# Gate rows of the last layer taken as row sums and carried through memory, and half of the last MLP's first products in plain fp32

## The chip, the cores and the metric

The kernel runs on one core of one Trainium2 chip. The metric is the device time of one execution in microseconds (us), lower is better. The median of three runs of the kernel before is 1636.49 us, from 1636.38 to 1636.56.

## The reference, cut to what matters

Two layers over 256 latent and 256 context tokens of width 1024. Layer 0 mixes tokens by a convolution module, layer 1 by a bidirectional mLSTM with four heads; behind each mixer stands an MLP with a squared ReLU. Every sub-layer is modulated and gated by six vectors that a linear map of the conditioning vector gives.

```python
sh1, sc1, g1, sh2, sc2, g2 = adaln(c[:, None, :], ada_w[i], ada_b[i])   # silu(c) @ w + b, cut in six
u = modulate(h, sh1, sc1)                                               # h * (1 + sc1) + sh1
...
h = layer_norm(ALPHA * h + g1 * y, ln1_g[i], ln1_b[i])
h = layer_norm(ALPHA * h + g2 * sq_relu_mlp(modulate(h, sh2, sc2), mlp_w1[i], mlp_w2[i]), ln2_g[i], ln2_b[i])
```

In layer 1 only the latent stream is needed at the end. What the change touches are g1 and g2 of layer 1, the denominators of the mLSTM's heads, and the first quarter of `u @ w1` of layer 1's MLP.

## The kernel before

All weights are float32 in memory. For the tensor engine each weight block is split into a high part `wh`, rounded to the engine's fp32r type by ScalarE (`split`, L155), and a low part `wl`, the rest, by VectorE (L156). A product is then three fp32r products: high by high, high by low, low by high (`mm3` L186 to L190, `mm3t` L224 to L226). In layer 1's MLP the activations `u2` lie as [high | low], 512 columns wide, so that one product with `wh` over 512 columns and one with `wl` over 256 columns do the same (`wide` L202, `wides` L213); `joined` adds the two halves. A product in plain fp32 (no split) is one instruction in the program and two matmul records in the trace.

Weights come through SyncE's queue in blocks of 1 MB into `raw`, a tile with three buffers (L149). A buffer is free when the split that reads it is done. The tile framework orders each engine's instructions with a scheduler of its own, which may move work far ahead of the place where it is written; `issue_after` and pinned order bind it.

**The six vectors of layer 1.** Units of 512 outputs are computed from `ada_w`. Units 0 to 3 and 6 to 9 (sh1, sc1, sh2, sc2) are made by VectorE (`AdaV.step`, L434): a multiply and row sum over a transposed weight block `ar` from `adaT_w`, two halves to a column of 128 outputs. Units 4 and 5 (g1) go in the same class another way (L442, L444): VectorE accumulates the weight rows scaled by the conditioning vector, and `AdaV.row` (L453 to L463) sums over the partitions with four products by a matrix of ones and adds the result to G1, which was loaded with the bias. Units 10 and 11 (g2) are made by the tensor engine in the last seam (`Ada.mm`, L356, 16 plain fp32 products 32 columns wide), and `gate2` (L2027 to L2032) spreads them over the partitions with four products.

**The attention stage.** `attend(h)` forms the numerators of head h, `denominators(h)` (L1711 to L1723) four products by a column of ones, an absolute value on ScalarE and a maximum and reciprocal on VectorE. It is called within `attend(h)` behind the first numerator. At the end of `attend(h)` stand eight transposes (L1823).

**The last seam.** When the residual `R` of the mLSTM is done (L1902, L1903), it is normalised (`ln1_rows`, L1927), transposed in four turns of four blocks (`turn`, L1961), and scaled and split into `u2` (L1967, L1978 to L1983). The 16 products of g2 are pinned between the turns. Then the first four output blocks of w1 run together (`wides`, eight steps of the contraction, in each four products over 512 and four over 256 columns), then blocks 4 and 5 (their weights split ahead into `wx`), 6, 7, and then w2's 16 half blocks of this chunk.

Of the kernel before, what the change touches and what calls it, by code (L numbers as in the profile page):

```python
# [71 lines left out]
def hybrid_kernel(ctx: ExitStack, tc: tile.TileContext, xT, vecs_d, taps_d, bdw_d, ada0_w, ada_w, adaT_w, wg_d, pw1a, pw1, pw2, w1_0, w2_0,  # L72
# [131 lines left out]
    def wides(pss, ws, rhs):  # L204

        n = rhs[0][0].shape[-1] // 2
        for kt in range(8):
            for low in (1, 0) if kt == 7 else (0, 1):
                for ps, w in zip(pss, ws):
                    w_, x_, o_ = kcol(w, kt)[low], rhs[kt][0], ps  # L210
                    if low:
                        x_, o_ = x_[:, :n], ps[:, :n]
                    nc.tensor.matmul(o_, w_, x_, start=kt == 0 and not low, stop=kt == 7 and not low)  # L213
# [23 lines left out]
    def gemm_steps(w_ap, groups, rhs, n, epi, ko=0, pre=None, spare={}, ahead=False):  # L237
# [25 lines left out]
        if ko:  # L263
            ws, pss = [], []
            for m in range(ko):
                g = groups[m // 2]
                if m not in pre:
                    if (g, 0) not in raws:
                        raws[g, 0] = raw_load(w_ap[g, 0])
                    pre[m] = split_w(raws[g, 0][:, (m % 2) * 1024:(m % 2 + 1) * 1024])  # L270
                ws.append(pre[m])
                pss.append(psum("mm" if m < 3 else "cv")[:, :n])
            if len(rhs[0]) == 1:
                wides(pss, ws, rhs)
# [138 lines left out]
    class AdaV:  # L413
# [4 lines left out]
        def __init__(self, l, units, streams, rows=()):  # L418
            self.l, self.units, self.streams, self.i, self.acc = l, list(units) + list(rows), streams, 0, []
            self.ncol, self.loads = len(units), []  # L420

        def step(self):
            n, kt = divmod(self.i - len(self.loads), DT)
            if n == len(self.units):
                return
# [3 lines left out]
            if n < self.ncol:  # L429
                b, half = divmod(kt, 2)  # L430
                col = 4 * self.units[n] + b
                for s in self.streams:
                    o = ada[self.l][:, col, s:s + 1]
                    nc.vector.tensor_tensor_reduce(tmp("S") if s == 0 else w, w, crow[s][half], 1.0,  # L434
                                                   o if half else V(f"ada_b{self.l}", col),
                                                   op0=ALU.mult, op1=ALU.add, accum_out=o)
                return
            if kt == 0:
                self.acc.append(tmp("S"))
            a, c = self.acc[-1], cs[:, kt, 14 + self.streams[0]:15 + self.streams[0]]  # L440
            if kt == 0:
                nc.vector.tensor_scalar(a, w, c, None, op0=ALU.mult)  # L442
            else:
                nc.vector.scalar_tensor_tensor(a, w, c, a, op0=ALU.mult, op1=ALU.add)  # L444

        def load(self):
            n, kt = divmod(self.i, DT)
            u = self.units[n]
            w = adp.tile([P, 512], F32, tag="ar", name=nm("ar"), bufs=2)
            nc.sync.dma_start(w, adaT_w[u - 2 * (u > 5), kt // 2, kt % 2] if n < self.ncol  # L450
                              else ada_w[self.l, u, kt // 4, :, kt % 4 * 512:kt % 4 * 512 + 512])
            self.i += 1
            return w  # L453

        def row(self, i, dst):

            parts = tmp("E", F32R), tmp("E", F32R)
            split(*parts, self.acc[i])
            ps = psum(("mm", "fl")[i])
            for k, part_ in enumerate(parts):  # L460
                nc.tensor.matmul(ps, ones_r, part_, start=k == 0, stop=k == 1)
            with tc.high_priority(-300):
                nc.vector.tensor_tensor(dst, ps, dst, op=ALU.add)  # L463
# [804 lines left out]
    ada_n1, ada_n2 = AdaV(1, range(4), (0, 1)), AdaV(1, range(6, 10), (1,), (4, 5))  # L1268
# [3 lines left out]
    def each1(c, m, s):  # L1272
        if c == 0 and m == 7 and s != 0:
# [3 lines left out]
            for k in range(4):  # L1277
                with tc.issue_after(loaded[0]):
                    nc.sync.dma_start(crow[k // 2][k % 2],
                                      rows_d[6 + k // 2:7 + k // 2, k % 2 * 512:k % 2 * 512 + 512].broadcast_to([P, 512]))  # L1280
# [167 lines left out]
    for _ in gemm_steps(wv, range(8), xm, T, v_epi):  # L1448
# [9 lines left out]
        if vstep > ET:  # L1458
            ada_n2.step()
# [176 lines left out]
    for p in range(2):  # L1636
        pair(p)
    rx = raw_load(wo[0, 0, 0])
# [72 lines left out]
    def denominators(h):  # L1711

        den, es = psum("ln"), sums[h]
# [20 lines left out]
    def gate_o(h):  # L1734

        for d in range(2):
# [5 lines left out]
            for q in range(4):  # L1742
# [3 lines left out]
                for i in range(2):  # L1746
                    w = ws[i] if ws else split_w(raw[:, i * 1024:(i + 1) * 1024])
                    for t in range(2):
# [6 lines left out]
                        if q == 3 and i == 1:  # L1755
                            og[h, d, t] = o_ = OG()
                            nc.vector.tensor_tensor(o_, pss[t], bo, op=ALU.add)
                            nc.scalar.activation(o_, o_, AF.Sigmoid)
# [13 lines left out]
    def attend(h):  # L1772
# [5 lines left out]
        for t in range(2):  # L1778
            for d in range(2):
# [7 lines left out]
                if h not in rden:  # L1787
                    denominators(h)
                    if h == H - 1:
                        with tc.issue_after(mark["abs"]):  # L1790
                            nc.scalar.activation(con.tile([P, 1], F32, name=nm("warm")), eps, AF.Sqrt)
# [25 lines left out]
        for jp in range(2):  # L1817
            tr = psum("ln")
            for jj in range(2):
                j = 2 * jp + jj  # L1820
                for t in (1, 0):
# [3 lines left out]
                    if jj == 0 and t == 1:  # L1825
                        lead = a.ins
            y = og[h, 1, jp]
# [109 lines left out]
    for main, side, per in Z.att:  # L1937
# [7 lines left out]
        for _ in side:  # L1945
            pass
    for g_ in range(2):
        rx = raw_load(w1_1[g_, 0])
        for m in range(2 * g_, min(2 * g_ + 2, 3 + Z.pre4)):
            pre1[m] = split_w(rx[:, (m % 2) * 1024:(m % 2 + 1) * 1024])  # L1950
    ca, cb = comb(1, "ln1_g1", "ln1_b1", "sc2", "sh2", (1,))
    ada_n3 = Ada(1, 10, 2)
    fold_r = con.tile([P, 16], F32R, name="fold_r")
    nc.vector.tensor_copy(fold_r, fold)
    u2 = [X(F32R) for _ in range(DT)]

    def turn(t, g_, tag="ln"):

        tr = psum(tag)
        for i in range(4):  # L1960
            nc.tensor.transpose(tr[:, i * P:(i + 1) * P], R[:, t, g_ * 512 + i * P:g_ * 512 + (i + 1) * P], ident)  # L1961
        return tr

    def lows(y, t, g_):
        for i in range(4):
            f = 4 * g_ + i
            nc.vector.tensor_tensor(u2[f][:, C + t * P:C + (t + 1) * P], y[:, i * P:(i + 1) * P],  # L1967
                                    u2[f].bitcast(F32)[:, BLK[t]], op=ALU.subtract)

    def ln1(tr, t, g_, vector=False, low=True, y=None, blocks=range(4)):  # L1970

        ts = BLK[t]
        y = y or tmp("SL"[vector])
        for i in blocks:
            f, sl = 4 * g_ + i, slice(i * P, (i + 1) * P)
            for o_ in (u2[f][:, ts], y[:, sl]):
                if vector:
                    nc.vector.tensor_scalar(o_, tr[:, sl], ca[:, 1, f:f + 1], cb[:, 1, f:f + 1],  # L1978
                                            op0=ALU.mult, op1=ALU.add)
                else:  # L1980
                    nc.scalar.activation(o_, tr[:, sl], AF.Identity, scale=ca[:, 1, f:f + 1], bias=cb[:, 1, f:f + 1])
            if low:
                nc.vector.tensor_tensor(u2[f][:, C + t * P:C + (t + 1) * P], y[:, sl], u2[f].bitcast(F32)[:, ts],  # L1983
                                        op=ALU.subtract)
        return y

    def ada_unit(blocks, kts=range(DT)):
        pin[0] = True
        ada_n3.mm(blocks, kts)
        pin[0] = False  # L1990

    units = [ada_load(1, 10)]
    with tc.issue_after(loaded[0]):
        units.append(ada_load(1, 11, PW))
    tr0 = turn(0, 0)
    y0 = ln1(tr0, 0, 0, low=False, blocks=range(2))
    tr1 = turn(0, 1, "cv")

    scaled = ln1_rows(1, True)
    with tc.issue_after(roots[0]):  # L2000
        ln1(tr0, 0, 0, low=False, y=y0, blocks=(2, 3))
    ada_unit(units[0])
    ada_unit(units[1], range(4))
    with tc.issue_after(scaled):
        lows(y0, 0, 0)
        ln1(turn(1, 0), 1, 0)
        tr2 = turn(1, 1)
        ada_unit(units[1], range(4, 8))
# [225 lines left out]
```

## Time and profile before

| what | value |
|---|---|
| median of three runs | 1636.49 us |
| the profiled execution | 1636.4 us |
| its span, first to last instruction | 1634.7 us |
| granted tensor engine clock, mean | 0.999 |
| busy: tensor engine, its weight loads | 99%, 83% |
| busy: VectorE, ScalarE, GpSimd | 66%, 45%, 1% |
| instructions | 22791 |

Times in the timeline count from the span's start. PE is the tensor engine's matmul, PEld its weight load, DVE VectorE, ACT ScalarE, SPq SyncE's queue. A timeline row gives start, length, engine, line, operation, written and read tiles, partitions by columns, and how many instructions are merged in it. The length of a matmul holds its latency; in a merged row the pitch is (row's length less one instruction's) by (count less one). The 1.7 us between the span and the execution's time lie outside the instructions.

### The profile page before, as it was taken

The page shows a single profiled execution, that of the slowest core. Times are in us where ns is not written, and L with a number is a line of the kernel's source. Part 1 is how long each engine was busy: PE and PEld are TensorE (multiplying, and loading weights), DVE is VectorE, ACT ScalarE, POOL GpSimd, SP SyncE. Part 2 cuts the span into 40 slices and gives each one's busy share as a digit, 9 for nine tenths or more (in the row PEclk, how much of TensorE's full clock was granted, in tenths as well). Part 3 has the DMA queues.
Part 4 walks back from the last instruction along what each step waited for, and adds up shares of the span by engine and source line. Part 5 has one row for each costly group of instructions (what it writes and reads, how often), then busy time and mean ns, then how long its engine had stood idle before and what let it go on. Part 6 is the DMA issues. An engine that isn't in the chain of part 4 may idle for free.

```text
span 1634.7 us, 22791 instructions
## 1 busy us (share of the span) xinstructions
PE 1624.8 (99%) x8758; PEld 1352.7 (83%) x8758; DVE 1071.5 (66%) x2013; ACT 732.9 (45%) x1176; POOL 15.3 (1%) x67
## 2 busy tenths in 40 slices
PE   9999999999999999999999999999999999999998
PEld 6675998888888998877787899888888888878887
DVE  7697896886635877862234643453489876786777
ACT  4314763232324585552223532443478654555453
POOL 0000000000000000000000000000000000000001
PEclk9999999999999999999999999999999999999999
DMA  9766323556523078697563622342556565675552
GB/s 359 257 219 245 104 104 135 172 195 213 174 91 142 23 236 258 199 302 229 194 226 139 248 106 103 130 180 104 177 204 229 209 223 206 235 294 182 181 198 85
DMA packets 88124, 306.87 MB, mean 188 GB/s; under 512 B 12844, under 2 KB 31184, under 8 KB 60112
## 3 DMA queue, kind: packets, MB, share of 16 engines
q1 hardware_dynamic: 65552, 289.12, 50.3%
q10 hardware_dynamic: 22464, 16.30, 3.1%
q8 instruction: 69, 1.13, 0.3%
q14 instruction: 39, 0.32, 0.1%
HBM read 287.52 MB, written 17.86 MB: 187 GB/s over the span
## 4 chain that ended last, share of the span: by engine, by line
PE 98%; DVE 1%; ACT 0%; issue 0%; DVEq 0%
PE mm L186 18%; PE mm L189 18%; PE mm L190 18%; PE mm L202 10%; PE mm L226 3%; PE mm L224 3%; PE mm L225 3%; PE cv L226 2%; PE cv L224 2%; PE cv L225 2%; PE fl L356 1%; PE ln L224 1%; PE ln L225 1%; PE ln L226 1%; PE fl L225 1%; PE fl L224 1%
## 5 line engine op out<-in xcount | busy, mean ns | idle before, releaser
L156 DVE TENSOR_TENSOR wl<-raw,wh 128x1024 fp32r<-128x1024 f32 x344 | 419.0, 1222 | 262.8 <-ACT wh L155 260.4
L155 ACT CAST wh<-raw 128x1024 fp32r<-128x1024 f32 x344 | 359.4, 1053 | 455.2 <-PE mm L189 275.3
L189 PE MATMUL mm<-u,wh 128*128 128x512 f32 (+1 forms) x802 | 288.7, 361 | 0.0
L186 PE MATMUL mm<-u,wh 128*128 128x512 f32 (+1 forms) x674 | 239.4, 356 | 0.0
L190 PE MATMUL mm<-u,wl 128*128 128x512 f32 (+1 forms) x674 | 238.2, 355 | 0.0
L189 PEld LDWEIGHTS mm<-u,wh 128*128 128x128 f32 x802 | 151.2, 189 | 23.0 <-issue 0.8
L186 PEld LDWEIGHTS mm<-u,wh 128*128 128x128 f32 x674 | 127.2, 189 | 20.5 <-issue 2.4
L190 PEld LDWEIGHTS mm<-u,wl 128*128 128x128 f32 x674 | 127.1, 189 | 18.5 <-issue 0.8
L186 PE MATMUL mm<-xm,wh 128*128 128x512 f32 x256 | 100.2, 391 | 0.0
L190 PE MATMUL mm<-xm,wl 128*128 128x512 f32 x256 | 99.6, 389 | 0.0
L186 PE MATMUL mm<-hid,wh 128*128 128x512 f32 (+1 forms) x256 | 93.0, 364 | 0.0
L189 PE MATMUL mm<-hid,wh 128*128 128x512 f32 (+1 forms) x256 | 92.8, 362 | 0.0
L190 PE MATMUL mm<-hid,wl 128*128 128x512 f32 (+1 forms) x256 | 92.7, 362 | 0.0
L224 PE MATMUL mm<-wh,xl 128*128 128x512 f32 x208 | 81.4, 393 | 0.0
L225 PE MATMUL mm<-wh,xl 128*128 128x512 f32 x208 | 81.1, 390 | 0.0
L226 PE MATMUL mm<-wl,xl 128*128 128x512 f32 x208 | 80.9, 392 | 0.0
L189 PE MATMUL mm<-qq,wh 128*128 128x272 f32 x256 | 73.9, 289 | 0.0
L186 PE MATMUL mm<-qq,wh 128*128 128x272 f32 x256 | 73.5, 288 | 0.0
L190 PE MATMUL mm<-qq,wl 128*128 128x272 f32 x256 | 73.5, 288 | 0.0
L1382 DVE SCALAR_TENSOR_TENSOR E<-pad,vecs,E 128x512 f32<-128x512 f32 x64 | 47.9, 748 | 19.3 <-ACT E L1380 18.2
L155 ACT CAST hid<-E 128x256 fp32r<-128x256 f32 (+1 forms) x70 | 34.0, 487 | 58.9 <-DVE E L1223 54.8
L156 DVE TENSOR_TENSOR rr<-mm,rr 128x256 fp32r<-128x256 f32 x64 | 27.0, 422 | 50.8 <-ACT rr L155 50.8
(600 smaller groups left out, 3267.4 us busy)
## 6 DMA issues: line engine op xcount, KB each, us to landing
raw<-w SPq DMA_DIRECT2D x64, 1024.0 KB, 4.8
raw<-wo SPq DMA_DIRECT2D x32, 1024.0 KB, 4.9
raw<-ada_w SPq DMA_DIRECT2D x22, 1024.0 KB, 6.4
ar<-adaT_w SPq DMA_DIRECT2D x64, 256.0 KB, 3.0
raw<-wv SPq DMA_DIRECT2D x16, 1024.0 KB, 6.6
raw<-wq SPq DMA_DIRECT2D x16, 1024.0 KB, 4.8
raw<-wk SPq DMA_DIRECT2D x16, 1024.0 KB, 4.8
u<-wqT SPq DMA_DIRECT2D x56, 256.0 KB, 5.4
```

The lines of the kernel that those rows point to most:

```text
L155: c = nc.scalar.copy(hi, src)
L156: lastsub[0] = nc.vector.tensor_tensor(lo, src, hi.bitcast(F32), op=ALU.subtract).ins
L186: a = nc.tensor.matmul(ps, wh, xh, start=start, stop=False)
L189: nc.tensor.matmul(ps, wh, xl, start=False, stop=False)
L190: lastmm[0] = nc.tensor.matmul(ps, wl, xh, start=False, stop=stop).ins
L202: nc.tensor.matmul(o_, w_, x_, start=start and i == 0, stop=stop and i == 15)
L224: nc.tensor.matmul(ps, xh, wh, start=start, stop=False)
L225: nc.tensor.matmul(ps, xl, wh, start=False, stop=False)
L226: return nc.tensor.matmul(ps, xh, wl, start=False, stop=stop).ins
L356: a = mark_unit[0] = nc.tensor.matmul(ps[32 * j:32 * j + 32], cs[:, kt, 14 - 2 * v:46 - 2 * v], blocks[kt], start=first and kt < 4, stop=l ...
L1382: nc.vector.scalar_tensor_tensor(s2_(acc), pad[:, :, k:k + C], V("w_conv", m * QTAP + k), s2_(acc), op0=ALU.mult, op1=ALU.add)
```

## The change

It has four parts.

1. `AdaV` makes all of units 6, 7, 8, 9, 4, 5, 10, 11 as row sums over transposed blocks, so the 16 accumulating steps of units 4 and 5 go and 32 row sums come. When the last is issued, `gate_rows` writes the two gates from `ada[1]` to memory (`g_dr`, two DMAs on ScalarE's queue, element by element), and G1 and G2 are loaded from there, spread over the partitions. `AdaV.row`, `gate2` and the products of `Ada` in the seam are gone.
2. In the last seam the first four contraction steps of output blocks 0 to 3 are plain fp32 products of the raw weights with the scaled rows (`whole32`), 32 of 128 columns. `wides` starts at step 4 on the same banks; its step 4 issues each high product as two of 256 columns. Only the second half of those weights is split.
3. `denominators(h + 1)` stands directly behind the transposes of head h, in a bank of `cv`.
4. The warming of the square root's table waits for the last sigmoid too.

```diff
-                    nc.tensor.matmul(o_, w_, x_, start=kt == 0 and not low, stop=kt == 7 and not low)
+                    elif kt == k0 > 0:
+                        for sl in (slice(0, n), slice(n, 2 * n)):
+                            nc.tensor.matmul(ps[:, sl], w_, x_[:, sl], start=False, stop=False)
...
-    ada_n1, ada_n2 = AdaV(1, range(4), (0, 1)), AdaV(1, range(6, 10), (1,), (4, 5))
+    g_dr = dp.tile([2, D], F32, name="g_dr")
+    def gate_rows():
+        for i, u in enumerate((16, 40)):
+            nc.scalar.dma_start(g_dr[i].rearrange("(k p) -> p k", p=P), ada[1][:, u:u + 8, 1])
+    ada_n1, ada_n2 = AdaV(1, range(4), (0, 1)), AdaV(1, (6, 7, 8, 9, 4, 5, 10, 11), (1,), gate_rows)
...
-    G1 = rows(qe.tile([P, D], F32, name="G1"), rows_d[0:1])
+    G1 = rows(qe.tile([P, D], F32, name="G1"), g_dr[0:1])
-    for i in range(2):
-        ada_n2.row(i, G1[:, HF[i]])
...
-        den, es = psum("ln"), sums[h]
+        den, es = psum("cv" if h else "ln"), sums[h]
...
+            if jp and h + 1 in sums:
+                with tc.issue_after(a.ins):
+                    denominators(h + 1)
...
-            pre1[m] = split_w(rx[:, (m % 2) * 1024:(m % 2 + 1) * 1024])
+            w32.append(rx[:, i * 1024:(i + 1) * 1024])
+            pre1[2 * g_ + i] = split_w(w32[-1][:, 512:1024])
...
+    def whole32(y, t, f):
+        for m in range(4):
+            a = nc.tensor.matmul(up4[m][:, BLK[t]], w32[m][:, f * P:(f + 1) * P], y[:, f * P:(f + 1) * P],
+                                 start=f == 0 and t == 0, stop=False)
...
-    ada_unit(units[0])
-    ada_unit(units[1], range(4))
+    for f in range(3):
+        a = whole32(y0, 0, f)
...
+        with tc.issue_after(mark["high"]), tc.issue_after(mark["low"]):
+            pre1[2, 0, m] = split_w(rx[:, m * 1024:(m + 1) * 1024], WX)
...
-            if c == 1:
-                gate2()
```

On the tensor engine, at the last seam, there stood before the following: transposes of `res` (the residual), then the products of g2 into `fl`.

```order
L1961 MATMUL ln_13078<-ident,res_10720 128x128 x4
L1961 MATMUL cv_13088<-ident,res_10720 128x128 x4
L356 MATMUL fl_13102<-raw_13058,cs 32x512 x4
L356 MATMUL fl_13102<-raw_13060,cs 32x512 x4
L356 MATMUL fl_13102<-pw_13062,cs 32x512
L356 MATMUL fl_13102<-pw_13064,cs 32x512
L356 MATMUL fl_13102<-pw_13066,cs 32x512
L356 MATMUL fl_13102<-pw_13068,cs 32x512
L1961 MATMUL ln_13119<-ident,res_10720 128x128 x4
L1961 MATMUL ln_13137<-ident,res_10720 128x128 x4
```

Four more of g2 follow, then `wides` from step 0. Now, from the second pair of turns on, there stands this (line 1952 is `turn`, 1976 `whole32`; `S_13098` holds the scaled rows of tokens 0 to 127, `S_13139` those of 128 to 255, `raw` the unsplit weights):

```order
L1952 MATMUL ln_13129<-ident,res_10769 128x128 x4
L1952 MATMUL fl_13134<-ident,res_10769 128x128 x4
L1976 MATMUL mm_13089<-S_13098,raw_13056 128x128
L1976 MATMUL mm_13090<-S_13098,raw_13056 128x128
L1976 MATMUL mm_13091<-S_13098,raw_13066 128x128
L1976 MATMUL cv_13092<-S_13098,raw_13066 128x128
L1976 MATMUL mm_13089<-S_13139,raw_13056 128x128
L1976 MATMUL mm_13090<-S_13139,raw_13056 128x128
L1976 MATMUL mm_13091<-S_13139,raw_13066 128x128
L1976 MATMUL cv_13092<-S_13139,raw_13066 128x128
```

Twelve plain products of `S_13098` stand between the first two turns and these rows, twelve more of `S_13139` behind them, then `wides` from step 4.

On the tensor engine, where the scores of the mLSTM end (`fl` from `rr`) and the output gates begin (`mm` from `wh` and `xl`), the four products of `AdaV.row` stood between:

```order
L190 MATMUL fl_9826<-rr_10627,xc_8098 128x512
L461 MATMUL mm_10725<-E_10721,ones 128x512
L461 MATMUL mm_10725<-E_10722,ones 128x512
L461 MATMUL fl_10733<-E_10729,ones 128x512
L461 MATMUL fl_10733<-E_10730,ones 128x512
L224 MATMUL mm_10791<-wh_10700,xl_10739 128x512
```

Now the gates follow the scores at once:

```order
L189 MATMUL fl_9874<-rr_10675,xc_8147 128x512
L190 MATMUL fl_9874<-rr_10674,xc_8147 128x512
L228 MATMUL mm_10824<-wh_10749,xl_10772 128x512
L228 MATMUL mm_10825<-wh_10749,xl_10772 128x512
L229 MATMUL mm_10824<-wh_10749,xl_10772 128x512
```

On SyncE's queue at the last seam (`raw<-w_1` are blocks of w1 and w2, `row` the five spread rows of the last normalisation and g2), it stood so before:

```order
L380 DMA pw_13076<-ada_w 128x512
L149 DMA raw_13183<-w_1 128x2048
L149 DMA raw_13353<-w_1 128x2048
L149 DMA raw_13424<-w_1 128x2048
L1659 DMA row_13178<-rows_d 128x1024
L1659 DMA row_13179<-rows_d 128x1024
```

Now the rows stand ahead of the last block of w1 (`raw_13349`) and the first of w2 (`raw_13416`), and these two take the buffers that `whole32` reads:

```order
L149 DMA raw_13211<-w_1 128x2048
L1650 DMA row_13206<-g_dr 128x1024
L1650 DMA row_13207<-rows_d 128x1024
L1650 DMA row_13208<-rows_d 128x1024
L1650 DMA row_13209<-rows_d 128x1024
L1650 DMA row_13210<-rows_d 128x1024
L149 DMA raw_13349<-w_1 128x2048
L149 DMA raw_13416<-w_1 128x2048
```

More of the change, by code (lines that the diff above doesn't have):

```diff
@@ L1637, in hybrid_kernel @@
         pair(p)
+    ada_n2.step()
     rx = raw_load(wo[0, 0, 0])
@@ L1965, in lows, with low @@
+    def low(y, t, g_):
         for i in range(4):
             f = 4 * g_ + i
[L1967 to L1974, printed above, removed]
-            f, sl = 4 * g_ + i, slice(i * P, (i + 1) * P)
[L1976 to L1984, printed above, removed]
-        return y
@@ L2000, in hybrid_kernel @@
     with tc.issue_after(roots[0]):
-        ln1(tr0, 0, 0, low=False, y=y0, blocks=(2, 3))
-    ada_unit(units[0])
-    ada_unit(units[1], range(4))
+        high(y0, 0, 0, tr0)
     with tc.issue_after(scaled):
[L2005 to L2008, printed above, removed]
-        ln1(tr1, 0, 1, True)
-        ln1(tr2, 1, 1)
+        with tc.issue_after(a):
+            tr2 = turn(1, 0)
+            tr3 = turn(1, 1, "fl")
+        y1 = plain(tr2, 0, tmp("S"))
@@ L2025, in rescale @@
                 tc.keep_in_program_order(nc.vector.scalar_tensor_tensor(r, i0, ALPHA, i1, op0=ALU.mult, op1=op))
-    def gate2():
-        for v in range(2):
-            ps = psum()
-            for k in range(2):
-                nc.tensor.matmul(ps, fold_r[:, 2 * v + 1:2 * v + 2].broadcast_to([P, P]), parts[k], start=k == 0, stop=k == 1)
-            nc.vector.tensor_tensor(G2[:, HF[v]], ps, G2[:, HF[v]], op=ALU.add)
     def finish(t):
```

136 lines of the change are left out of this document (72 added, 64 removed).

## The prediction

> **What bounds the kernel now.** I read the page first, then the tensor engine's waits, then the timeline at each place that the change touches. The page's first line, busy us by engine:
>
> ```profile
> PE 1624.8 (99%) x8758; PEld 1352.7 (83%) x8758; DVE 1071.5 (66%) x2013; ACT 732.9 (45%) x1176; POOL 15.3 (1%) x67
> ```
>
> The tensor engine is busy for 1624.8 of 1634.7 us. Of its waits in the middle of the program, the view of waits names this one for the change's places:
>
> ```profile
> PE fl L461 <- ACT x L1513: 0.2, 1, 0.2
> ```
>
> So the time is the tensor engine's queue laid end to end. Only what shortens that queue, or opens a gap in it, moves the time; VectorE, ScalarE and the DMAs count where they make it wait. I therefore add up the tensor engine's time at three places, and then look for new gaps. The largest place is the last seam:
>
> ```profile
> 1442.81 0.60 PE L1961 MATMUL ln<-ident,res 128*128 128x128 f32 x4
> 1443.24 0.60 PE L1961 MATMUL cv<-ident,res 128*128 128x128 f32 x4
> 1443.77 1.92 PE L356 MATMUL fl<-raw,cs 128*32 128x512 f32 x16
> 1445.51 1.04 PE L356 MATMUL fl<-pw,cs 128*32 128x512 f32 x8
> 1446.65 1.18 PE L1961 MATMUL ln<-ident,res 128*128 128x128 f32 x8
> 1447.75 1.07 PE L356 MATMUL fl<-pw,cs 128*32 128x512 f32 x8
> 1448.75 0.97 PE L213 MATMUL mm<-x,wh 128*128 128x512 f32 x3
> ...
> 1450.26 0.86 PE L213 MATMUL mm<-x,wh 128*128 128x512 f32 x3
> ...
> 1451.66 0.86 PE L213 MATMUL mm<-x,wh 128*128 128x512 f32 x3
> ...
> 1460.06 2.96 PE L202 MATMUL fl<-x,wx 128*128 128x512 f32 x16
> ```
>
> It lasts from 1442.81 to 1460.06, 17.25 us. The products of g2 (L356) cover the time in which the rows are normalised and scaled. The first step of `wides` takes 1.51 us (1448.75 to 1450.26), a later one 1.40 (1450.26 to 1451.66).
>
> **Part one, the seam: 2.2 us less.** 16 products of g2 and four of the eight steps go; 32 plain fp32 products of 128 columns come, 64 records. Their price is in the trace: the warm-up products by `ones`, plain fp32, 128 by 128 by 128.
>
> ```profile
> L180 PEld LDWEIGHTS mm<-ones x4: 186/190/192, 7.3 to 7.7; 128*128 128x128 f32 x4
> 7.34 0.52 PEld L180 LDWEIGHTS mm<-ones 128*128 128x128 f32 x4 [0.41 <-issue]
> ```
>
> Two products are four records; (0.52 - 0.19) / 3 = 0.11 us a record, 0.22 us a product. The eight transposes give the same pitch from another stationary block each time: of the row at 1443.24 the next row starts 0.53 later for four. I take 0.111; the upper bound is 0.120, the pitch of the 256-column products that I work out from a step: 1.40 us for four of 512 at 0.23 and four of 256.
>
> The Trainium skill's page "TensorE: Matmul & The Clock Gate", section "Weight-path perf modes — Fast Weight Load (FWL) and DoubleRow", says that the fast weight load is on only where the input is not FP32, which speaks against plain products on 128 columns: each would bring its own slow load. Its section "LDWEIGHTS (loading the stationary operand)" gives columns by 1.2 in ns, 107 for 128; an estimate from that page, with each of 64 loads added to its product, is 6.8 us more and a time of 1639.9. The warm-up row does not show such a sum.
>
> What the other engines do there sets whether the products can start:
>
> ```profile
> 1443.44 0.46 ACT L1981 ACTIVATE x<-ln,cb,ca 128x128 fp32r<-128x128 f32 x1 [1.21 <-PE ln L1961]
> 1445.43 0.30 ACT L1912 ACTIVATE mv<-mv,eps 128x1 f32<-128x1 f32 x1 [0.48 <-DVE mv L1911]
> 1445.63 0.44 ACT L1981 ACTIVATE x<-ln,cb,ca 128x128 fp32r<-128x128 f32 x1
> 1445.96 1.00 DVE L1927 TENSOR_SCALAR res<-res,mv 128x512 f32<-128x512 f32 x2
> 1447.68 0.41 DVE L1978 TENSOR_SCALAR x<-cv,ca,cb 128x128 fp32r<-128x128 f32 x1
> 1448.00 0.41 DVE L1978 TENSOR_SCALAR L<-cv,ca,cb 128x128 f32<-128x128 f32 x1
> 1452.82 0.71 ACT L155 CAST wx<-raw 128x512 fp32r<-128x512 f32 x1
> 1454.78 1.89 DVE L156 TENSOR_TENSOR wx<-raw,wx 128x512 fp32r<-128x512 f32 x3
> ```
>
> I step through it. ScalarE's first scaled block is there at 1443.44 + 0.46 = 1443.90. The transposes end at about 1443.7, so the tensor engine waits 0.3 to 0.4 and starts at 1444.05. Twelve products, 24 x 0.111 = 2.7, to 1446.7; VectorE has the second half of the rows at 1446.96, so the eight transposes (0.9) run to 1447.6. Four products to 1448.5. By then ScalarE, which takes 0.345 a block, has done four high parts from 1445.63 and needs the third turn (1447.35) for the first block of the second rows: 1447.8, ahead of need. The other 16 products run to 1452.05. Step 4 needs the third and fourth turn scaled and split: VectorE's eight scalings at 0.32 from 1446.96 end at 1449.6, ScalarE's eight behind 1448.8 at 1451.6, the differences (0.2 each) of step 4 at about 1451.0, of step 7 at 1451.9. So `wides` doesn't wait. It takes 4 x 1.40 + 0.11 for the first step + 0.05 for the split high products: 1457.8. The seam shrinks by 1460.06 - 1457.8 = 2.2 us. VectorE's last differences end at 1452.9, so the casts into `wx` start where they did (1452.82) and end by 1456.5, 1.3 us ahead of the tensor engine.
>
> **Part two, g2's spread: 0.93 us less.**
>
> ```profile
> 1515.34 0.39 PE L2031 MATMUL mm<-S,fold_r 128*128 128x512 f32 x1
> ...
> 1516.27 0.39 PE L224 MATMUL ln<-wh,hid 128*128 128x512 f32 x1
> ```
>
> The four products of `gate2` take 1516.27 - 1515.34. They stand in a full queue, what follows is split long before, so the whole of it goes.
>
> **Part three, g1's row sums: 0.1 us less, not 1.4.**
>
> ```profile
> 1173.34 0.63 PE L461 MATMUL mm<-E,ones 128*128 128x512 f32 x2
> 1174.03 1.93 ACT L155 CAST xl<-raw 128x256 fp32r<-128x256 f32 x6
> 1174.46 2.86 DVE L156 TENSOR_TENSOR xl<-raw,xl 128x256 fp32r<-128x256 f32 x8 [6.40 <-ACT xl L155]
> 1174.75 0.63 PE L224 MATMUL mm<-wh,xl 128*128 128x512 f32 x2
> 1175.22 0.39 PE L225 MATMUL mm<-wh,xl 128*128 128x512 f32 x1
> ```
>
> They hold the engine from 1173.34 to 1174.75, 1.41 us. But the next product needs the first `xl`, whose high part VectorE finds at 1174.46 and whose low part is there at about 1174.9. ScalarE casts it right behind the four scalings of the scores, in the same order as before. So the gate's first product can start at 1174.65 and the third at 1175.1: a wait takes the row sums' place, and 0.1 is left (bounds 0 and 1.41).
>
> **Part four, the denominators and the rest: nothing.** The four products are the same:
>
> ```profile
> 1403.36 0.95 PE L1716 MATMUL ln<-ones,F 128*128 128x1 f32 x8
> 1404.17 0.47 PE L224 MATMUL cv<-wh,pw 128*128 128x512 f32 x1
> ```
>
> 0.81 us a head before and behind the transposes; beside transposes a change between kinds of product is saved, at most 0.1 a head (0.47 against the 0.39 of the next), so between -0.3 and +0.2 in all, and I take 0. The sums are done heads ahead, and the tensor engine does not wait for a denominator now.
>
> On VectorE 32 row sums come and 16 accumulating steps go. The scheduler puts the new ones into layer 0's MLP:
>
> ```profile
> L434 DVE CUSTOM_DVE_ANT_0 ar<-ar,L,vecs x32: 743/750/753, 262.2 to 427.1; 128x512 f32<-128x512 f32 x32
> 300.00:320.00 20.00, 20.00 (x90) 16.55 (x89) 18.73 (x41) 7.18 (x10) 0.00 (x0) 1.00 0.62 203
> 480.00:500.00 20.00, 20.00 (x90) 16.57 (x89) 9.73 (x12) 8.42 (x12) 0.00 (x0) 1.00 0.23 75
> ```
>
> 32 x 0.83 (0.75 and a read of 0.08) = 27 us, on 440 to 500 us where VectorE is busy half the time or less. In the row for 300 to 320 it is busy 18.73 of 20 us with the tensor engine's 20.00 untouched: that is the cover, and so I cost this at nothing. The two gate DMAs wait on ScalarE's queue for the last row sums with casts queued behind them; these casts have 2 us and more of idle time ahead of each. G1 is read some 650 us later.
>
> **The sum.** 2.2 + 0.93 + 0.1 = 3.25 us, from the profiled execution's 1636.4 (the median is 1636.49): 1633.1. About 0.2%, 3.3 us, is what a measurement of this kernel can tell from no change; the forecast lies at that bound. Its own spread: 64 x 0.009 = 0.6 for the record's pitch, 0.3 for the denominators, 0.2 for the start: 1632.4 to 1634.0.
>
> **The rivals.**
>
> *Weights late behind the seam.* `whole32` reads `raw` until 1451.6 and 1452.05, so the last block of w1 and the first of w2 are asked for only then.
>
> ```profile
> 1436.16 9.92 SPq L149 DMA_DIRECT2D raw<-w  x3
> 1464.20 1.23 DVE L156 TENSOR_TENSOR wl<-raw,wh 128x1024 fp32r<-128x1024 f32 x1
> 1465.68 0.42 DVE L219 TENSOR_TENSOR E<-mm,E 128x256 f32<-128x256 f32 x1
> DMA to landing us min/median/max: 4.2/4.9/11.4
> ```
>
> Before, all three were asked for by 1446.1. At the median the two land at 1456.5 and 1457; the w2 split on VectorE (1464.20, less 2.2) needs it at 1462 with its cast ahead. At the longest, 11.4, it lands at 1463.5, and VectorE, in order, comes 3 to 4 us late to the `joined` at 1465.68, which frees the bank for block 7 with some 2.3 us to spare. Up to 1.5 us of the gain goes: 1634.6. Chance 0.12.
>
> *The row sums go whole.* If the casts of `xl` came earlier, 1.3 more: 1631.8. Their order on ScalarE is unchanged. Chance 0.05.
>
> *Slower: plain products bound by their weight loads.* In the warm-up rows the stationary block is always `ones`; here each product has another. If the load (0.19) is not hidden, a record costs 0.30, 64 x 0.19 = 12.2 more: 1645.3. It decides from a record of 0.21 on (6.5 us over 64). Against it: transposes keep 0.11 with changing blocks. Chance 0.05.
>
> *VectorE late in layer 0*, a few us either side of the bound, against the cover above: 0.03, of it 0.02 slower.
>
> **How the numbers follow.** The forecast has 0.75, of it 0.43 beyond 0.2%. Faster 0.43 + 0.05 = 0.48; within 0.2% 0.32 + 0.12 + 0.01 = 0.45; slower 0.05 + 0.02 = 0.07. The range reaches from 1632.0 (the forecast's spread and a little of the row sums) to 1635.6, the late weights at twice their price.
>
> **What would show it.** Right: the seam from the first transpose to block 4's first product takes about 15 us with 64 records at 0.11 after one wait of 0.3; at the scores' end the tensor engine stands about 1.2 us for `xl`; no L2031 row; no wait in 1452 to 1475. Wrong: records above 0.12, a wait for `x` at step 4, for `wh` at blocks 6 or 7, or in 440 to 510.

## The result, and the profile after

The changed kernel takes 1650.45 us (median of five, 1648.82 to 1651.58), against 1636.49 before: ratio 1.0084, with a 95% interval of 1.0069 to 1.0099. It is slower by 14 us, where 3.3 us less were forecast. The profiled execution took 1650.45 us, its span is 1648.7 us, 14.0 more than before.

The page's first line, and the tensor engine's waits inside the program:

```profile
PE 1623.7 (98%) x8754; PEld 1356.6 (82%) x8754; DVE 1077.0 (65%) x2052; ACT 728.1 (44%) x1173; POOL 15.2 (1%) x67
```

```profile
PE mm L186 <- ACT hid L155: 13.3, 2, 12.1
PE mm L228 <- ACT xl L155: 1.0, 1, 1.0
PE mm L189 <- DVE hid L156: 0.7, 2, 0.3
```

The work of the tensor engine has shrunk by 1.1 us, but there is a wait of 12.1 us that was not there. It lies in layer 0's MLP, as the windows show (columns: us of the window, then busy time of PE, PEld, DVE, ACT, POOL, the granted clock, DMA share, GB/s):

```profile
500.00:520.00 20.00, 19.90 (x95) 16.56 (x93) 14.79 (x28) 8.98 (x15) 0.00 (x0) 1.00 0.46 143
520.00:540.00 20.00, 6.01 (x25) 5.12 (x25) 8.11 (x14) 5.86 (x10) 0.00 (x0) 0.58 0.67 170
540.00:560.00 20.00, 20.00 (x153) 19.95 (x153) 10.01 (x25) 3.13 (x8) 0.00 (x0) 0.91 0.10 41
```

Here the tensor engine is busy 6 of 20 us and its clock falls to 0.58. To see where the whole difference comes from, I laid the tensor engine's products of both traces side by side and took the shift, start after less start before:

| place | forecast | shift gained or lost |
|---|---|---|
| ahead of layer 0's MLP | 0 | -0.2 |
| layer 0's MLP, 519.6 to 543.9 us | 0 | +19.1 |
| the row sums' place ahead of the gates | -0.1 | -0.2 |
| from the first gate to the last seam | 0 (-0.3 to +0.2) | -1.4 |
| the last seam | -2.2 | -2.35 |
| `gate2` | -0.93 | -0.92 |
| sum | -3.25 | +14.0 |

All places but one came out as worked out, or better. Layer 0's MLP, costed at nothing, cost 19.1 us (the expectations below put it at 18.8). The timeline of the changed kernel shows how (line 1257 is the gates' write to memory, 446 the load of `ar`, 149 that of a weight block). ScalarE first, then the tensor engine:

```profile
516.70 0.37 ACTq L1257 DMA_DIRECT2D g_dr<-ada  x1
531.34 1.14 ACT L155 CAST u<-raw 128x512 fp32r<-128x512 f32 x2 [10.23 <-DMA raw<-w]
```

```profile
533.04 0.58 PE L186 MATMUL mm<-hid,wh 128*128 128x256 f32 x1 [12.10 <-ACT hid L155]
533.93 0.58 PE L189 MATMUL mm<-hid,wh 128*128 128x256 f32 x1 [0.31 <-DVE hid L156]
534.32 0.41 PE L190 MATMUL mm<-hid,wl 128*128 128x256 f32 x1
534.53 0.41 PE L186 MATMUL mm<-hid,wh 128*128 128x256 f32 x1
```

ScalarE waits 10.2 us for the last weight block of this MLP; a cast of `hid` stands behind it in ScalarE's order, and the tensor engine waits for that `hid`. Then the products of 256 columns start 0.21 us apart (534.32 to 534.53), where a full clock gives 0.12, until 543.9. The four waits in this stretch sum to 14.0 us. Of the other 5.1 some 3.3 are the slower pitch; the rest stands around the waits, where the first product takes 0.58 us instead of 0.28. Why was the block late? SyncE's queue of the changed kernel (`w` are the MLP's blocks of 1 MB):

```profile
496.63 9.85 SPq L446 DMA_DIRECT2D ar<-adaT_w  x5
507.28 0.33 SPq L149 DMA_DIRECT2D raw<-w  x1
508.55 1.71 SPq L446 DMA_DIRECT2D ar<-adaT_w  x2
518.43 0.33 SPq L149 DMA_DIRECT2D raw<-w  x1
```

And of the kernel before:

```profile
507.45 0.33 SPq L149 DMA_DIRECT2D raw<-w  x1
509.28 82.86 SPq L149 DMA_DIRECT2D raw<-up_z  x8
```

The block was asked for at 518.43 instead of 507.45, and it took 12.8 us to land instead of 4.7 (answers for these single transfers: before, then after):

```profile
DMA to landing us min/median/max: 4.7/4.7/4.7
```

```profile
DMA to landing us min/median/max: 12.8/12.8/12.8
```

So 11.0 us of lateness come from the issue and 8.1 from the transfer. Beside the transfer runs the second of the two gate writes, issued at 516.70, 1024 elements of 4 bytes. In the view of DMAs for 516 to 532 us (q10 is ScalarE's queue):

```profile
GB/s 0 0 0 0 6 4 0 0 0 0 61 0 0 0 20 102 102 61 20 0 61 41 61 41 20 41 0 61 0 61 61 287 369 410 348 410 389 430 451 410
q10 hardware_dynamic: 1040, 0.00, 3.0%
raw<-w SPq DMA_DIRECT2D x1, 1024.0 KB, 12.8
raw<-up_z SPq DMA_DIRECT2D x1, 1024.0 KB, 14.1
g_dr<-ada ACTq DMA_DIRECT2D x1, 4.0 KB, 11.1
```

The write is 1040 packets, so nearly every packet is one element. The 4 KB take 11.1 us, to 527.8, and the two blocks beside them take 12.8 and 14.1. The line of rates has 40 slices of 0.4 us: while the write is under way no slice shows more than 102 GB/s, and from 528.4 on they show 287 to 451. So the blocks move for the most part once the write is done. What in the DMA engines makes them so slow until then, no run here shows.

The last seam went as worked out. Its first and last rows, with line 1952 the transposes, 1976 the plain products, 215 the first split product and 202 block 4:

```profile
1460.13 0.60 PE L1952 MATMUL ln<-ident,res 128*128 128x128 f32 x4
1461.27 0.94 PE L1976 MATMUL mm<-S,raw 128*128 128x128 f32 x6
1469.32 0.95 PE L215 MATMUL mm<-x,wh 128*128 128x256 f32 x6
1475.04 2.96 PE L202 MATMUL fl<-x,wx 128*128 128x512 f32 x16
```

From the first transpose to the first plain product it is 1.14 us, of which 0.3 is the wait for the scaled rows; `wides` starts 9.19 us in (worked out: 9.24) and block 4 at 14.91 (15.0).

### The profile page after: what moved, and what is told of

Read it like the earlier page. It is cut to its first block, busy times and chain, and to the rows that moved or that the text cites. A ratio compares the mean times of both kernels' runs of the same rounds, so it can differ in the third digit from the quotient of the medians.

```text
span 1648.7 us, 22836 instructions
## 1 busy us (share of the span) xinstructions
PE 1623.7 (98%) x8754; PEld 1356.6 (82%) x8754; DVE 1077.0 (65%) x2052; ACT 728.1 (44%) x1173; POOL 15.2 (1%) x67
## 4 chain that ended last, share of the span: by engine, by line
PE 90%; DMA 6%; DVE 3%; issue 1%; ACT 0%; DVEq 0%; SPq 0%; ACTq 0%
PE mm L186 15%; PE mm L189 15%; PE mm L190 15%; PE mm L202 10%; DMA ar<-adaT_w 4%; PE mm L228 4%; PE mm L230 3%; PE mm L229 3%; PE cv L230 2%; PE cv L228 2%; PE cv L229 2%; PE fl L360 1%; DMA raw<-w 1%; DVE ar L439 1%; PE ln L228 1%; PE ln L229 1%
## 5 line engine op out<-in xcount | busy, mean ns | idle before, releaser
L156 DVE TENSOR_TENSOR wl<-raw,wh 128x1024 fp32r<-128x1024 f32 (+1 forms) x344 | 416.5, 1215 | 255.4 <-ACT wh L155 250.5
L155 ACT CAST wh<-raw 128x1024 fp32r<-128x1024 f32 (+1 forms) x344 | 357.0, 1045 | 458.8 <-PE mm L189 269.0
L186 PE MATMUL mm<-hid,wh 128*128 128x512 f32 (+1 forms) x256 | 95.1, 372 | 13.4 <-ACT hid L155 13.3
L189 PE MATMUL mm<-hid,wh 128*128 128x512 f32 (+1 forms) x256 | 94.8, 370 | 0.7 <-DVE hid L156 0.7
L186 PEld LDWEIGHTS mm<-hid,wh 128*128 128x128 f32 x256 | 50.1, 196 | 21.6 <-ACT hid L155 14.1
```

The costliest lines, as they stand in the source:

```text
L155: c = nc.scalar.copy(hi, src)
L156: lastsub[0] = nc.vector.tensor_tensor(lo, src, hi.bitcast(F32), op=ALU.subtract).ins
L186: a = nc.tensor.matmul(ps, wh, xh, start=start, stop=False)
L189: nc.tensor.matmul(ps, wh, xl, start=False, stop=False)
```

## The experiments

Several theories were open. **Theory one** at first: in SyncE's queue the 32 new loads wait for one of two buffers that VectorE frees, and the blocks of w behind them come late; the writes of the gates make the last one worse. **Rivals**: VectorE is held in its own order by row sums that wait for their data; or the volume of loads and row sums costs this wherever it stands; or the writes alone do it. Each time below has the kernel before measured beside it on the same chip (1636.7 to 1636.9 us).

**The loads moved out of layer 0** (`e1_held`).

```diff
-            nc.sync.dma_start(w, adaT_w[...])
+            with tc.issue_after(loaded[0]) if n >= 4 else nullcontext():
+                nc.sync.dma_start(w, adaT_w[...])
```

> The changed kernel with the 32 loads of the last four units (4, 5, 10, 11) each queued on SyncE behind the weight block that stands before it in the program, so that loads and row sums fall in the mLSTM stage (600 to 1170 us) and not in layer 0's MLP. Theory one (in SyncE's queue the new loads wait for a buffer that VectorE frees, and the blocks of w behind them come late): the shift of 18.8 us in layer 0's MLP is gone, 1650.5 - 18.8 = 1631.7, between 1630.5 and 1633. Theory two (32 loads of 256 KB and 27 us of row sums cost this much wherever they stand): above 1640.

Measured: 1640.12 us, ratio 1.0021 (1.0012 to 1.0030). This is far above theory one's range and at the lower edge of theory two's. In the trace layer 0's MLP loses nothing any more, and 10 us come back, but a new wait stands at 904 us, and with its lower clock it shifts all that follows by 7.7 us:

```profile
PE mm L202 <- DVE xc L156: 4.9, 1, 4.9
```

VectorE's timeline there:

```profile
900.26 0.75 DVE L439 CUSTOM_DVE_ANT_0 ar<-ar,L,ada 128x512 f32<-128x512 f32 x1 [4.13 <-DMA ar<-adaT_w]
907.17 0.75 DVE L439 CUSTOM_DVE_ANT_0 ar<-ar,L,vecs 128x512 f32<-128x512 f32 x1 [6.15 <-DMA ar<-adaT_w]
907.85 2.77 DVE L156 TENSOR_TENSOR xc<-raw,xc 128x256 fp32r<-128x256 f32 x8
```

Two row sums wait 4.1 and 6.2 us for their blocks, and the splits of `xc` that the tensor engine needs stand behind them. So a row sum that waits does hold VectorE's order, which is the rival. The two gate writes stand here at 973 and 1135 us. A block of 1 MB asked for beside the first, at 978.57, took 9.9 us where 4.8 is the median, but nothing needed it earlier.

**Only the gate writes put off** (`e2_gates_late`).

```diff
-            nc.scalar.dma_start(g_dr[i]...)
+            with tc.issue_after(anchors[-1]):
+                nc.scalar.dma_start(g_dr[i]...)
```

> The changed kernel with the two DMAs that write the gates element by element queued on ScalarE behind the mLSTM's last weight cast, everything else in its place. Theory one, as I read the trace: the last block of w is issued late (518.43) by the loads ahead of it, and lands 12.9 us later instead of 4.9 because the elements (2080 packets in that stretch) fill the DMA engines; without them it lands 8 us earlier, the wait of 12.1 us falls to about 4, and the time to 1650.5 - 8 - some of the clock's 4.7 = 1638 to 1643. Rival: the elements are harmless and the late issue alone sets the wait: 1648 to 1652.

Measured: 1638.67 us, ratio 1.0013 (1.0004 to 1.0022), 11.8 us less than the changed kernel with 32 loads and row sums where they were. Ten single times lie between 1636.46 and 1642.15; the profiled one took 1642.06, so its trace shows one of the two slowest. Its waits:

```profile
PE mm L186 <- DVE wgq L1518: 2.4, 1, 2.4
PE mm L186 <- ACT hid L155: 2.0, 1, 2.0
```

In the MLP a wait of 2.0 us is left, and 3.5 us of shift. The last block of w is asked for at 512.54 and lands in 5.8 us. The other wait is new and stands where the writes are now: issued at 1147.4, they lie beside a block of `wo`, and ScalarE waits 9.1 us for it.

```profile
1163.93 1.05 ACT L155 CAST wh<-raw 128x1024 fp32r<-128x1024 f32 x1 [9.14 <-DMA raw<-wo]
```

That block took 14.1 us to land. The harm goes where the element writes go.

**The loads on another queue** (`e5_pool`).

```diff
-            nc.sync.dma_start(w, adaT_w[...])
+            (nc.gpsimd if n >= 4 else nc.sync).dma_start(w, adaT_w[...])
```

> The changed kernel with the 32 loads of the last four units on GpSimd's DMA queue, so that no block of w stands behind them; the row sums stand on VectorE as in the changed kernel. Theory one (SyncE's queue is held): the blocks of w are issued ahead again and most of 18.8 us goes, 1632 to 1640, the upper end if the writing of the gates still delays a transfer. Rival (VectorE is held: row sums that wait for their data stand ahead of the splits that the tensor engine needs): 1645 to 1655.

Measured: 1653.75 us, ratio 1.0111 (1.0096 to 1.0127). Theory one falls in this form. With no load of `ar` on SyncE's queue, the last block of w is asked for even later, at 526.08:

```profile
526.08 0.33 SPq L149 DMA_DIRECT2D raw<-w  x1
```

```profile
495.30 0.75 DVE L439 CUSTOM_DVE_ANT_0 ar<-ar,L,ada 128x512 f32<-128x512 f32 x1 [4.19 <-DMA ar<-adaT_w]
495.98 1.22 DVE L156 TENSOR_TENSOR wl<-raw,wh 128x1024 fp32r<-128x1024 f32 x1
```

VectorE's row sums wait for their data, the split of a weight block stands behind, and only that split frees the `raw` buffer that the next block needs. SyncE's order was not needed; VectorE's order was enough. The element writes are still in this run, and they have their part: its longest such wait, 9.1 us up to 485.65, stands beside the first of them, issued at 473.7.

**The denominators alone** (`e4_den`), the kernel before with parts three and four of the change:

```diff
+            if jp and h + 1 in sums:
+                with tc.issue_after(a.ins):
+                    denominators(h + 1)
```

> The kernel before with the denominators of heads 1 to 3 moved behind the transposes of the head ahead, in a bank of cv, and with the table's warming behind the last sigmoid; nothing else changed. My prediction: no change, 1636.5 (1636.2 to 1636.8). Rival, from the shift between the two traces, which falls by some 0.6 us from head 0 to the seam: 1635.9.

Measured: 1637.07 us, ratio 1.0000 (0.9991 to 1.0008). No difference that can be measured; in the traces the span is 0.3 us shorter.

**The gates in rows of 128 bytes** (`e6_rows32`): the decisive one. The loads stay as they are, and the form of the writes changes. Their time changes too: one transpose needs the row sums of both gates, so all eight writes go out from 513.5 us on, where the elements went at 468.7 and 516.7.

```diff
-        for i, u in enumerate((16, 40)):
-            nc.scalar.dma_start(g_dr[i].rearrange("(k p) -> p k", p=P), ada[1][:, u:u + 8, 1])
+        t = con.tile([P, 32], F32, name="gt")
+        nc.vector.transpose(t, ada[1][:, 16:48, 1])
+        for i in range(2):
+            for q in range(4):
+                nc.scalar.dma_start(g_dr[i].rearrange("(k q r) -> q k r", q=4, r=32)[q],
+                                    t[32 * q + 24 * i:32 * q + 24 * i + 8, :])
```

> The changed kernel with the gates turned on VectorE first (one 32 by 32 block transpose of 128x32) and written as 64 rows of 128 bytes in eight DMAs, where there were 2048 elements of 4 bytes in two; they are issued at the same place, and the 32 loads stand where they stood. Theory one, sharpened by the run with the writes put off (the elements hold up the block of 1 MB beside them by 8 to 10 us): the wait of 12.1 us falls to about 2, some 1.5 is left of the clock's loss, and nothing waits at 1160: 1636.5, between 1635 and 1638.5. Rival (the block is late because it is issued late): 1645 to 1651.

Measured: 1634.43 us, ratio 0.9989 (0.9980 to 0.9998): 16.0 us less than the changed kernel, 2.3 less than the kernel before, and a little below theory one's range. The tensor engine's longest wait in the MLP is now

```profile
PE mm L186 <- ACT hid L155: 1.5, 1, 1.5
```

and SyncE's queue asks for the last block at 512.21:

```profile
500.72 0.33 SPq L149 DMA_DIRECT2D raw<-w  x1
512.21 0.33 SPq L149 DMA_DIRECT2D raw<-w  x1
```

```profile
515.21 1.05 ACT L155 CAST wh<-raw 128x1024 fp32r<-128x1024 f32 x1 [1.77 <-DMA g_dr<-gt]
517.13 0.62 ACT L155 CAST u<-raw 128x512 fp32r<-128x512 f32 x1 [0.38 <-DMA raw<-w]
```

ScalarE casts the block at 517.13, so with the eight writes beside it it landed within 4.9 us, close to the 4.7 before the change. That is the test of the form. The wait that is left, 1.5 us, does not come from this block: its chain runs through the cast at 515.21, which stands behind the issue of four of the eight writes on ScalarE.

This run also parts the 11.0 us of late issue. With the loads and no element write ahead of it the block is asked for 4.8 us late (512.21 less 507.45), and with the writes put off at 512.54, in a trace that runs 1.3 us later by then, so 3.8 us late. The other 6.2 came from the first element write, at 468.7 us. The changed kernel's chain of waits and VectorE's timeline show it:

```profile
473.35 11.03 DMA ar<-adaT_w
```

```profile
484.40 0.75 DVE L439 CUSTOM_DVE_ANT_0 ar<-ar,L,vecs 128x512 f32<-128x512 f32 x1 [7.57 <-DMA ar<-adaT_w]
```

A load of 256 KB beside that write took 11.0 us, where the run with 128-byte rows has a median of 2.9 for these loads from 440 us on, and VectorE stood for it.

**The elements alone** (`e9_elements`), on the kernel before, with the loads as they were:

```diff
+        if c == 3 and m == 4:
+            for i in range(2):
+                with tc.issue_after(mark["relu"]):
+                    nc.scalar.dma_start(e_dr[i].rearrange("(k p) -> p k", p=P), ada[1][:, 0:8, 1])
```

> The kernel before with nothing changed but two writes added: 128x8 numbers each, element by element, to a scratch row in memory, on ScalarE's queue at about 503 us, just ahead of the last block of w in layer 0's MLP. It prices the elements alone, with that block issued in time. Theory one: the block lands 8 us later than its 4.9, some 4 of that is slack: 1638 to 1642. Rival (the elements alone are harmless, only with the late issue they cost): 1636.3 to 1637.3.

Measured: 1642.14 us, ratio 1.0034 (1.0021 to 1.0048), 5.4 us more, just above theory one's range and far from the rival's. The two writes take 12.8 us each, and the block of w, asked for in time at 507.93, is there only at 518.7 (10.8 us):

```profile
518.82 1.14 ACT L155 CAST u<-raw 128x512 fp32r<-128x512 f32 x2 [4.73 <-DMA raw<-w]
```

In this trace 5.0 us of shift arise in the MLP. Some 2 more arise at 1233 us, from a wait of 0.9 us for a weight's split and a lower clock behind it, which I can't tie to the writes.

**The loads spread over the value projection** (`e7_placed`), with 128-byte rows:

```diff
+            with tc.issue_after(vraws[self.i - 32]) if n >= 4 else nullcontext():
+                nc.sync.dma_start(w, adaT_w[...])
...
         vstep += 1
+        vraws.append(loaded[0])
```

> The same with the gates as rows of 128 bytes, and the 32 loads bound to the 32 groups of the value projection (668 to 870 us), one load behind each group's weight block, where VectorE is busy a third of the time. Theory one: layer 0's MLP loses nothing, no new wait comes, and the forecast's own sum is left: 1632.0, between 1631 and 1633.5. Rival (row sums that wait for their data hold VectorE's order wherever they stand, as at 900 us in the run with held loads): 1636 to 1641.

Measured: 1640.40 us, ratio 1.0021 (1.0012 to 1.0030). The rival was right again: a wait of 5.1 us that ends at 781.6 us, and 2.9 us more of shift with the lower clock behind it.

```profile
PE mm L190 <- DVE wl L156: 5.1, 1, 5.1
```

```profile
760.32 0.75 DVE L441 CUSTOM_DVE_ANT_0 ar<-ar,L,ada 128x512 f32<-128x512 f32 x1 [12.62 <-DMA ar<-adaT_w]
774.27 0.75 DVE L441 CUSTOM_DVE_ANT_0 ar<-ar,L,vecs 128x512 f32<-128x512 f32 x1 [2.43 <-DMA ar<-adaT_w]
779.67 0.75 DVE L441 CUSTOM_DVE_ANT_0 ar<-ar,L,ada 128x512 f32<-128x512 f32 x1 [1.30 <-DMA ar<-adaT_w]
780.35 1.22 DVE L156 TENSOR_TENSOR wl<-raw,wh 128x1024 fp32r<-128x1024 f32 x1
```

VectorE is idle two thirds of the time there, and it does not help. One row sum waits 12.6 us for its block, later ones up to 5.5, and the `wl` that the tensor engine needs is split only at 780.35, behind the last of them. Idle VectorE time in a window is no cover for an instruction that stands in order and waits.

**The seam without plain products** (`e8_noplain`), on the kernel just told: `turn`, scalings and eight steps of `wides` as before the change, without g2.

```diff
-    for f in range(3):
-        a = whole32(y0, 0, f)
...
-             spare={} if c else {4: "fl"}, begun=None if c else up4)
+             spare={} if c else {4: "fl"})
```

> The kernel with placed loads and 128-byte gate rows, with the last seam put back: all eight steps of the first four blocks from split weights, no plain products, and no products of g2 either. My reading: the first step can't start before the second tokens' rows are normalised, turned and split, so the tensor engine waits where the products of g2 stood, and the seam takes its old 17.0 us or so: 2 to 2.5 us slower than the kernel with placed loads. Rival: the splits for the first step come sooner without the plain products' own scalings, and the fewer records (12.8 us of steps and transposes) win: 1 us faster to 1 us slower than that kernel.

Measured: 1644.49 us, ratio 1.0044 (1.0032 to 1.0057), 4.1 us above the kernel with plain products. In the trace the seam takes 19.5 us, 4.6 more than with them and 2.3 more than before:

```profile
1446.22 0.60 PE L1958 MATMUL ln<-ident,res 128*128 128x128 f32 x4
1450.39 1.94 PE L1958 MATMUL ln<-ident,res 128*128 128x128 f32 x8 [3.14 <-DVE res L1927]
1465.74 2.50 PE L202 MATMUL fl<-x,wx 128*128 128x512 f32 x14
```

The tensor engine waits 3.1 us for the second tokens' rows, and then runs at a lower clock: eight transposes take 1.94 us, where eight took 1.18 before. The plain products are the cover that g2 was. I had the direction, and missed the clock.

**The last loads behind w** (`e10_wfirst`), on the kernel with 128-byte rows:

```diff
+            with tc.issue_after(mark["w_last"]) if n >= 4 and self.i >= 56 else nullcontext():
                 nc.sync.dma_start(w, adaT_w[...])
```

> The kernel with 128-byte gate rows, and the last 8 of the 32 loads queued on SyncE behind the last block of w of layer 0's MLP, so that the last three blocks of w have no load between them. Theory one: the loads' own part (the last block of w issued at 512 instead of 507.5 us, a shift of 1.6 us in the MLP) goes: 1.6 us below the run with 128-byte rows alone, 1632.8, between 1632 and 1634. Rival (the 8 row sums that now wait on VectorE in 520 to 560 us hold the residual's work there): the same 1634.4 or up to 3 us more.

Measured: 1634.07 us, ratio 0.9982 (0.9973 to 0.9991). The MLP's wait is 0.2 us, but 0.7 us come back at 544 us, for the residual's norm on VectorE. There ScalarE's squares for this norm wait 1.4 us twice behind the issue of the eight gate writes, which now stand at 540 us:

```profile
PE ln L532 <- DVE ln L520: 0.7, 1, 0.7
```

Both halves of the expectation hold in part; 0.4 us between two runs with spreads of 3 us decide nothing.

**The first casts of xl sooner** (`e11_xlfirst`), on that kernel:

```diff
-            split(t[:, LO], t[:, HI], rx[:, j * C:(j + 1) * C])
+            with tc.high_priority():
+                split(t[:, LO], t[:, HI], rx[:, j * C:(j + 1) * C])
```

> The kernel with the last 8 loads behind w, and the first casts of xl given priority, so that they stand ahead of the last of the four scalings of the scores on ScalarE. My reading of part three (the wait of 1.0 us for xl at the head of the gates is ScalarE's order): the wait falls by one scaling's 0.55 to 0.7 us and the time with it, 0.6 below the kernel with the last loads behind w. Rival: the cast waits for something else, or the late scaling holds its bank for the gates' next products: no change or up to 0.5 slower.

Measured: 1633.50 us, ratio 0.9979 (0.9970 to 0.9988), the lowest median of all, 3.4 us below the kernel before. The 0.6 us to the run above are as expected, but the two intervals overlap. What decides is the trace, where the wait at the gates' head halves:

```profile
PE mm L228 <- ACT xl L155: 0.5, 1, 0.5
```

## Why the prediction was wrong, step by step

**The bound.** The time is the tensor engine's queue, and only gaps or a shorter queue move it: right. All 14 us are gaps, the lower clock behind them and a shorter queue.

**The seam** (-2.2 worked out, -2.35 measured): right, in its parts too. A record of the plain products takes 0.111 us with a new stationary block each time, so the slower rival did not occur: `wides` starts where the steps put it, 9.19 us in. The Trainium skill's page "TensorE: Matmul & The Clock Gate", section "Weight-path perf modes — Fast Weight Load (FWL) and DoubleRow", names 128 FP32 columns as a case without the fast load; the run shows that the load is hidden all the same here. There was no wait behind the seam for late weights.

**`gate2`** (-0.93, measured 14.97 to 14.05 in shift): right. **The row sums' place** (-0.1, measured -0.2): right, and the run with the casts sooner shows that the wait is ScalarE's order. **The denominators** (0): right, as the run of them alone shows. From the gates to the seam 1.4 us went, 1.1 beyond my bound, and that is luck. Some 0.5 of it lies around the gates' cumulative sums at 1191 us, where the products stand in another order, and 0.4 shows in the trace of the denominators alone too. Why is not settled.

**The step that failed** is in part four: "that is the cover, and so I cost this at nothing. The two gate DMAs wait on ScalarE's queue for the last row sums with casts queued behind them". It has two faults, and a smaller one: the first of the two writes did not wait for the last row sums but went out at 468.7 us. Among the signs of being wrong stood a wait in 440 to 510 us; the wait came just behind, from 521 to 533.

First, I weighed the issue of the gate writes on ScalarE and not the transfer. The two writes of 1024 elements land 11 to 12 us after their issue, and the transfers asked for beside them land some 8 us later than otherwise: 12.8 us instead of 4.7 for 1 MB, 11.0 instead of 2.9 for 256 KB. Writing rows of 128 bytes instead gave 16.0 us; adding the elements to the kernel before cost 5.4. The Trainium skill's page "DMA: Bandwidth & Descriptors", section "Rules for kernel authors", says that a strided last dimension becomes one descriptor per element and should be rearranged, and its section "Issuing engines are not separate DMA queues" that transfers issued by different engines run on the same 16 DMA engines and interleave. Both agree with this trace (1040 packets on ScalarE's queue, a block on SyncE's queue held up), and both could have been read ahead of the prediction.

Second, the 32 loads. I costed the row sums by their busy time against idle time of VectorE and priced no load. Without an element write ahead of it the last block is asked for 3.8 to 4.8 us late. That cost 3.5 us of shift in the trace with the writes put off, and at most 1.6 in the one with 128-byte rows, where the issue of the eight writes has a part in it. It is VectorE's order that does it, as the run with another queue shows: a row sum waits for its block, a weight's split waits behind it, and the buffer of the next block is free only after that. The two faults add up to more than their parts. In the MLP the elements alone shift 5.0 us, the loads alone at most 3.5, both together 19.1; the elements alone had no row sum to hold up ahead of the last block. Before, that block landed at 507.45 + 4.7 = 512.2 us; with the elements alone it lands at 518.7, 6.5 later, with both at 531.2, 19.0 later. The tensor engine's waits there sum to 3.0 and 14.0 us. So the first 3.5 to 5 us of lateness are slack; what lies beyond is paid in full, and then in clock.

**The rival** "VectorE late in layer 0, a few us either side" named the place and half of the mechanism, at a chance of 0.03 and with no price for the writes. A loss of 19 us there was in no rival.

## What to carry to other kernels

Price a moved or added DMA by its packets and by the transfers that run beside it, not by its issue: 2048 elements of 4 bytes cost more here than all else in the change gained, and one block transpose on VectorE with 128-byte rows took nearly all of the cost away. Their eight issues still take time of the engine that issues them. An instruction that waits for data in an in-order queue costs its wait to all that stands behind it, so the idle share of an engine in a window is no cover for it; look up what stands behind, and which buffer that frees. When a change with several parts comes out slower, lay the two traces side by side and take the shift by place: one table showed here that all places but one were good.

## What the runs showed that I had not expected

A wait of the tensor engine costs more than its length. After 12.1 us of waiting, products of 256 columns started 0.213 us apart until 543.8 us, 6 us past the last wait, and 14.0 us of waits became 19.1; after 3.1 us in the seam without plain products the clock was 0.68 over the next 10 us. By the clock records of the traces, inside the program, the tensor engine has half its clock for 3.41 us behind waits of 2.0 to 2.5 us, for 6.83 us behind those of 3.1, 4.9 and 5.1 us, and for 20.48 us in the changed kernel's MLP: always a multiple of 3.41. Length alone does not decide, since the wait of 1.5 us with 128-byte rows brought no lower clock and the one of 0.9 us with the elements alone did. The time of the changed kernel also scatters more: 2.8 us over five executions where the kernel before has 0.2 beside it (and 1.1 over 27 in a later measurement), and 2.5 to 5.7 us over ten or eleven in the variants with the 32 loads, with or without element writes.
